# One step later for the scaling of head outputs, and the last output projection as seven products on sums

## The chip, the cores and the metric

The kernel runs on one core of a Trainium2 chip. Its time is the device time of one execution in microseconds (us); before the change the median of three runs is 1851.86 us (1851.43 to 1857.75). The core has a matrix engine (TensorE, PE in the profile), which multiplies a 128x128 tile of weights with up to 512 columns, and three engines for the rest: VectorE (DVE), ScalarE (ACT) and GpSimd (POOL). SyncE (SP) issues every DMA of this kernel, in one order that is fixed when the program is built.

## The reference

A decoder layer on x of 2048 tokens by 1024 channels, all in float32:

```
h        = rms_norm(x, g_pre) * (1 + scale(c)) + shift(c)
pv, pg, hq, hf, hi, hg, mgp, mgh = split(h @ w_in)
branch_a = (pool(pv) @ pool_w * pool_scale * silu(pg)) @ w_pool_o
o        = hgrn2(silu(hq), 1 - f, hi, log f)      # 8 heads of 128, chunks of 64 tokens
branch_b = (rms_norm_per_head(o) * silu(hg)) @ w_hgrn_o
merged   = sigmoid(mgp) * branch_a + sigmoid(mgh) * branch_b
y        = merged @ w_out
x        = x + gate(c) * rms_norm(y, g_post)
```

## The kernel before

The tokens are worked in two passes (p = 0, 1) of 1024, each in two halves (t = 0, 1) of 512 columns, and a half in four tiles (tk) of 128 tokens. A float32 factor is split into a high and a low part that the matrix engine takes at full rate (`split`: ACT casts the high part, DVE subtracts it), and each product is made of three matmuls: high with high, high with low, low with high.

A pass has five stages: the values `hi` for all heads (`v_job`, results in `psV`); eight heads; the projection of branch A (`a_job`, `psA`); the projection and merge of branch B (`b_job`, `psB`, eight jobs j of 128 channels); and the output projection (`y_job`, `psy`). In pass 1 the output projection is four jobs, one for each half of the tokens t and of the output columns nn, and each has 8 blocks k of channels by 4 token tiles by 3 matmuls: 384 matmuls of 512 columns in all.

In a head, three pairs of blocks of `w_in` (tags fq, gp and m) are each made by `quad`: a 2x2 block product over two halves of the channels and two halves of the tokens, in seven products on sums in place of eight. The products leave PSUM in turn; the fourth is copied by ACT (L496, into the bank `pdm`, `pdgp` or `pdfq`), and further matmuls are then added to that bank. Between the products `tick()` moves the two running `hgrn` generators of the head before by one `yield`. Near its end, `hgrn` squares and sums the head output `po` in four tiles of 128 columns (L687, `junk`, sums in `ss`), POOL makes 1/sqrt of `ss` (two small instructions, L390 the second), ACT scales `po` into `on` (L692, four instructions), PE transposes `on` into `pot` three yields later (L698), and DVE and ACT turn it into factors of `b_job`.

Weights come through `take()`, which prepares them LOOK = 4 products ahead. In pass 0 they are loaded, summed and split on DVE and ACT (L172), and the split parts are stored in DRAM scratch (`keep`, L107, from SP). In pass 1 they are loaded back from there (`again`, L194, tag whl, 512 KB in one DMA, one of four buffers). The rows of x for the residual sum are loaded (xr, 256 KB each) in the second quarter of each job with nn = 1.

`y_job` at its end squares each bank on ACT for the row sum (L893, `jy`), multiplies it by the output gate on DVE (L390, `y`), and, when both column halves are there, DVE adds the sums (L902), POOL takes the power (`yss`), and DVE makes y times `yss` plus x (L911). Of the very last token tile ACT and POOL do one of the two halves (L908). The results are stored at once in the last job.

The order on each engine comes from the order in which the code issues its instructions and from a scheduler that places them by the buffers and results they need.

Of the kernel before, what the change touches and what calls it, by code (L numbers as in the profile page):

```python
# [8 lines left out]
F32 = mybir.dt.float32  # L9
# [24 lines left out]
MASK_W = P + 2 * 64 + 5 * NT * 64  # L34
NU = 76
GAP = 5
KINDS = (("m", "gp"), ("gp", "m"))


# [30 lines left out]
def tile_block(ctx: ExitStack, tc: tile.TileContext, x, c, w_ada, b_ada, g_pre, g_post, w_in,  # L70
# [137 lines left out]
    def quad_items(key, oa, ob, keep_it):  # L208
# [37 lines left out]
            return [f0, f1, f2, f3, lambda: one(4, "21"), lambda: one(5, "12"), lambda: one(6, "22")]  # L246
        items.append((7, make))

    early = {}
    pending = []  # L250

# [41 lines left out]


    psa = [ph.tile([P, T], F32, tag=f"ph{i}", name=f"psa{i}") for i in range(2)]
    shv = cst.tile([P, 8], F32, name="shv")
    scv = cst.tile([P, 8], F32, name="scv")

# [90 lines left out]
    def tt(o, a, b, op=MUL, e=None):  # L389
        return (e or V).tensor_tensor(o, a, b, op=op)  # L390
# [131 lines left out]
    def hgrn(p, h, t, cx):  # L522
# [270 lines left out]
        cx["V"][h] = vt  # L793


    def two_out(nm, p, i, t, src, cx, stay):
# [42 lines left out]
    def b_job(p, j, cx):  # L839
        ps = [bank(f"psB{p}_{j}_{t}") for t in range(2)]  # L840
        sm = sig_in(p, j, 1, cx)
        for half in range(2):
            w = take()
            for t in range(2):
                three(ps[t], w, [cx["gG"][4 * half + i, t] for i in range(4)], half == 0, half == 1)
        for t in range(2):
            a, b = cx["a"].pop((j, t)), sm[t]
            tt(b, ps[t], b)
            tt(a, a, b, op=ADD)
            hi, lo = utile(f"mgh{p}_{j}_{t}", F32R), utile(f"mgl{p}_{j}_{t}", F32R)  # L850
            split(a, hi, lo)
            cx["mg"][j, t] = (hi, lo)
# [9 lines left out]
    def y_job(p, t, nn, q, cx):  # L862
# [36 lines left out]
        for tk in range(NT):  # L899
# [5 lines left out]
            for n2 in (0, 1):  # L905
# [9 lines left out]
                else:  # L915
                    outs.append(o)


    cxs = []
    for p in range(NPASS):  # L920
        cx = {k: {} for k in ("sm", "F", "Q", "G", "V", "pw", "Gd", "Pd", "Sd", "gP", "gG", "a", "mg", "x", "xc", "h32",
                              "mv", "y", "yss")}
        cx["Vd"] = dram(f"Vd{p}", [P, 8, D])
        for h in range(NH):
            cx["Gd"][h] = dram(f"Gd{p}_{h}", [P, 2, 2, T])
        for g in range(NG):
            cx["Pd"][g] = dram(f"Pd{p}_{g}", [P, 2, 2, T])
        for j in range(KT):
            for w in range(2):
                cx["Sd"][j, w] = dram(f"Sd{p}_{j}_{w}", [P, 2, T])  # L930
        cxs.append(cx)

    def krow(src, k, o):
        return src[k * P:(k + 1) * P, o:o + T]

    for p in range(NPASS):
        for t in range(2):
            for grp in range(2):
                for k in range(KT):
                    plain_item(("v", grp, k), krow(w_in, k, O_I + grp * T), None, t == 1)  # L940
# [13 lines left out]
        for t in range(2):  # L954
# [50 lines left out]
    for p in range(NPASS):  # L1005
# [3 lines left out]
        if p == 0:  # L1009
# [13 lines left out]
        vj = [(t, grp, q) for t in range(2) for grp in range(2) for q in range(4)]  # L1023
        if p == 0:
            vj = vj[4:]
        for n, (t, grp, q) in enumerate(vj):
# [8 lines left out]
                once(mixes)  # L1035
        while mixes:
            once(mixes)

        v_head(p, 0, cx)
        for h in range(NH):  # L1040
# [17 lines left out]
            steps = []  # L1058

            def tick_in():  # L1060
                tick()
                once(steps)

            quad("fq" + n, cx, fq, tick)
            active.extend(hgrn(p, h, t, cx) for t in range(2))
            tick()
            for i, kind in enumerate(KINDS[h == NH - 1]):
                if kind == "gp":
                    quad("gp" + n, cx, gp, tick)
# [5 lines left out]
                tick()  # L1075
            if p + 1 < NPASS:
                x_stats(8 + h)

        for j in range(KT):
            if j > 0:  # L1080
# [21 lines left out]
        for t in range(2):  # L1102
            for nn in range(2):
                for q in range(4):
                    y_job(p, t, nn, q, cx)
# [29 lines left out]
```

## Time and profile before

| | before |
|---|---|
| median of three runs | 1851.86 us |
| the profiled execution | 1851.48 us |
| its span | 1849.7 us |
| PE busy | 1782.6 us, 96% of the span |
| DVE, ACT, POOL busy | 1089.1, 799.9 and 80.0 us |
| mean DMA rate | 240 GB/s |

The span runs from the first instruction to the last; the execution's own time is 1.8 us more. PE counts as busy while a matmul is under way; matmuls overlap, so a row's mean duration is more than the step from one matmul to the next. The stages of the span: heads of pass 0 lie between 160 and 740 us, most of the heads of pass 1 between 1050 and 1480, the output projection of pass 1 between 1750.46 and 1839.11, and the span ends at 1849.70.

### The profile page before, as it was taken

To read this page: it belongs to the slowest core of one execution; us is meant where nothing else is said; L and a number is where in the kernel's file an instruction comes from. 1 tells how busy PE (TensorE), PEld (TensorE's weight loads), DVE (VectorE), ACT (ScalarE), POOL (GpSimd) and SP (SyncE) were. 2 spreads that over 40 slices of the span, in tenths; PEclk is the share of its full clock that TensorE was granted. 3 is DMA by queue.
4 is the path that set the end of the run, shared out by engine and by line. 5 is a ranking of instruction groups with operands and counts; after the bars stand their busy time and mean duration, and the time that the engine had idled before them with its cause. 6 is when DMAs were issued, how large, how long until landed. Compare 5 with 4: busy or idle time off the path is not lost.

```text
span 1849.7 us, 31713 instructions
## 1 busy us (share of the span) xinstructions
PE 1782.6 (96%) x12053; PEld 1456.7 (79%) x12053; DVE 1089.1 (59%) x2328; ACT 799.9 (43%) x1863; POOL 80.0 (4%) x136
## 2 busy tenths in 40 slices
PE   5999999999999999999999999999999999999997
PEld 4788878878888777787788778878888788788886
DVE  7568877887888884565432255465455456533322
ACT  4746656656556562223322335445344344311111
POOL 1100000000000000000000000000000000000000
PEclk9999999999999999999999999999999999999999
DMA  8697676676767759987887765664764764694476
GB/s 298 233 322 277 221 268 243 231 261 225 266 241 246 247 201 320 361 288 255 295 310 242 246 193 175 224 206 154 234 205 159 231 201 162 233 340 163 141 258 230
DMA packets 236530, 444.19 MB, mean 240 GB/s; under 512 B 18989, under 2 KB 109786, under 8 KB 236378
## 3 DMA queue, kind: packets, MB, share of 16 engines
q1 hardware_dynamic: 236378, 442.17, 69.9%
q8 instruction: 95, 1.56, 0.3%
q14 instruction: 57, 0.47, 0.1%
HBM read 269.61 MB, written 172.49 MB: 239 GB/s over the span
## 4 chain that ended last, share of the span: by engine, by line
PE 79%; ACT 6%; DMA 3%; DVE 3%; POOL 2%; issue 2%; SPq 1%; POOLq 0%; DVEq 0%; ACTq 0%
PE psB L278 9%; PE psV L278 8%; PE psy L278 8%; PE pafq L278 6%; PE pagp L278 6%; PE pam L278 5%; PE pefq L278 5%; PE psA L278 4%; PE pegp L278 4%; PE pem L278 3%; PE psa L278 3%; PE pbfq L278 2%; PE pbm L278 2%; PE pdfq L278 2%; PE pdm L278 2%; PE pbgp L278 2%
## 5 line engine op out<-in xcount | busy, mean ns | idle before, releaser
L172 DVE TENSOR_TENSOR whl<-wr,whl 128x512 fp32r<-128x512 f32 x210 | 143.7, 689 | 83.6 <-ACT whl L172 82.6
L172 ACT CAST whl<-wr 128x512 fp32r<-128x512 f32 x210 | 129.8, 620 | 128.6 <-DMA wr<-in_w_hgrn_o_dram 22.4
L278 PE MATMUL psy<-whl,mgh 128*128 128x512 f32 x512 | 160.1, 393 | 1.4 <-DVE y L390 0.7
L278 PE MATMUL psV<-whl,hB 128*128 128x512 f32 x512 | 161.3, 397 | 0.1
L278 PE MATMUL psB<-Gh,whl 128*128 128x512 f32 x512 | 158.6, 390 | 0.0
L578 DVE COPY_PREDICATED PT<-mask,psa 128x256 f32<-128x256 uint8 x160 | 86.1, 548 | 51.5 <-PE psa L278 51.5
L278 PEld LDWEIGHTS psy<-whl,mgh 128*128 128x128 f32 x512 | 95.0, 188 | 22.5 <-DMA whl<-scr_y 1.7
L278 PEld LDWEIGHTS psB<-Gh,whl 128*128 128x128 f32 x512 | 96.1, 188 | 20.5 <-issue 0.5
L278 PEld LDWEIGHTS psV<-whl,hB 128*128 128x128 f32 x512 | 96.6, 191 | 19.8 <-ACT V L787 0.3
L278 PE MATMUL psV<-whl,lB 128*128 128x512 f32 x256 | 100.8, 395 | 0.0
L278 PE MATMUL psB<-Gl,whl 128*128 128x512 f32 x256 | 100.0, 391 | 0.0
L278 PE MATMUL psy<-whl,mgl 128*128 128x512 f32 x256 | 100.0, 391 | 0.0
L278 PE MATMUL pam<-hT,whl 128*128 128x512 f32 x256 | 87.2, 402 | 0.0
L278 PE MATMUL pagp<-hT,whl 128*128 128x512 f32 x256 | 86.1, 397 | 0.0
L278 PE MATMUL psA<-Ph,whl 128*128 128x512 f32 x256 | 82.6, 397 | 3.4 <-DVE sm L390 1.7
L278 PE MATMUL pafq<-hT,whl 128*128 128x512 f32 x256 | 84.0, 389 | 0.0
L390 DVE TENSOR_TENSOR K<-K,TT 128x256 f32<-128x256 f32 x192 | 81.2, 424 | 1.0 <-PE psa L278 0.9
L278 PEld LDWEIGHTS psa<-X,K 128*32 128x32 f32 x2816 | 50.1, 110 | 29.8 <-issue 21.1
L172 ACT CAST mgh<-sm 128x512 fp32r<-128x512 f32 x32 | 19.7, 620 | 121.3 <-DVE sm L390 121.3
L390 DVE TENSOR_TENSOR y<-psy,gg 128x512 f32<-128x512 f32 x32 | 21.9, 688 | 73.9 <-ACT jy L893 73.7
L278 PE MATMUL psa<-X,K 128*32 128x48 f32 (+2 forms) x2816 | 61.0, 208 | 2.1 <-DVE PT L572 2.1
L572 DVE COPY_PREDICATED PT<-mask,psa 128x256 f32<-128x256 uint8 (+1 forms) x96 | 51.9, 541 | 18.3 <-PE psa L278 18.3
(358 smaller groups left out, 4307.5 us busy)
## 6 DMA issues: line engine op xcount, KB each, us to landing
wr<-in_w_in_dram SPq DMA_DIRECT2D x122, 256.0 KB, 4.4
whl<-scr_y SPq DMA_DIRECT2D x48, 512.0 KB, 4.4
sm<-Sd SPq DMA_DIRECT2D x64, 256.0 KB, 4.3
whl<-scr_v SPq DMA_DIRECT2D x32, 512.0 KB, 3.4
wa<-in_w_ada_dram SPq DMA_DIRECT2D x32, 256.0 KB, 5.4
x<-in_x_dram SPq DMA_DIRECT2D x32, 256.0 KB, 5.5
Vd<-V SPq DMA_DIRECT2D x32, 256.0 KB, 2.4
scr_v<-whl SPq DMA_DIRECT2D x16, 512.0 KB, 2.8
```

The source lines that it names most:

```text
L172: return A.copy(hi, src32), V.tensor_tensor(lo, src32, hi.bitcast(F32), op=SUB)
L278: PE.matmul(o, lhsT=l, rhs=r, start=start, stop=stop, skip_group_check=True)
L390: return (e or V).tensor_tensor(o, a, b, op=op)
L572: V.copy_predicated(dst.rearrange("p (c a) b -> p c a b", c=NT), m.unsqueeze(1).broadcast_to(shp), src.unsqueeze(2).broadcast_to(shp))
L578: V.copy_predicated(dst.rearrange("p (c q) a b -> p c q a b", c=NT), m, src.rearrange("p c (a b) -> p c a b", b=b).unsqueeze(2) .broadcast ...
```

## The change

There are two edits.

In `hgrn` one `yield` is moved from behind the scaling of `po` to a place ahead of it. The transposing into `pot` is issued at the same tick as before; the four scalings are issued one tick later.

The output projection of pass 1 is made as a 2x2 block product too, over the even and the odd 128-row blocks of w_out (2i and 2i+1), the two halves of its columns and the two halves of the tokens. Seven products on sums take the place of eight: B11, B21, T1, T2, T3, B22, T4, each of 4 blocks i by 4 token tiles by 3 matmuls, 336 in all. The sums of the merged branches (T1 to T4) are made in `b_job` of pass 1, on DVE, and split in `step` between the products. The seven sums of w_out are made in `row_factors` during the heads of pass 1: 56 steps, of which `htick` runs one at every second tick; they load w_out (16 DMAs of 256 KB), subtract or add (32 DVE instructions on 128x256), split (56 casts on ACT, 56 subtractions on DVE, 128x256) and store the parts to DRAM scratch (56 stores, from SP). `rows7` loads them back, 28 loads of 512 KB where there were 32, and adds the products on DVE and ACT as their banks become ready. Token half 1 is complete with B22, and half 0 with T4. The flag FAST_V is False, and what it guards is not built.

```
@@ hgrn
         tt(ss, ss, mh[:, 0:NT], op=ALU.pow, e=G)
+        yield
         on = utile("on" + n)
         for cc in range(NT):
             A.activation(on[:, cc * P:(cc + 1) * P], po[:, cc, :], AF.Copy, scale=ss[:, cc:cc + 1])
-        yield
         yield
         yield
@@ new function
+    def row_factors(key, src):
+        steps = []
+        W = T // 2
+        for i in range(4):
+            for c0 in (0, W):
+                r = {}
+                def put(f, nm, i=i, c0=c0, r=r):
...
+                    split(r[nm], hi, lo)
...
+                    store((key, f, i), scr[key, f, i].rearrange("p (z n) -> p z n", z=2)[:, :, c0:c0 + W],
+                          w.bitcast(F32).rearrange("p (z n) -> p z n", z=2))
...
+                steps += [ld, nop, lambda two=two: two((0, "11"), (1, "12")),
+                          lambda two=two, a=sums: two(a, (2, "s1")),
+                          lambda two=two, a=sums2: two(a, (3, "11")),
+                          lambda two=two, a=sums3: two((4, "21"), a),
+                          lambda two=two: two((5, "12"), (6, "22"))]
+        return steps
@@ new function
+    def rows7(name, mv, got, step):
+        acc = [bank(f"ra{name}{tk}") for tk in range(NT)]
+        c, s, u = ([utile(f"r{z}{name}{tk}") for tk in range(NT)] for z in "csu")
+        def done(nm, tk, ps):
+            if nm == "B11":
+                A.copy(c[tk], ps)
+            elif nm == "B21":
+                tt(c[tk], ps, c[tk], op=ADD)
+                got(0, 0, tk, c[tk])
+            elif nm == "T1":
+                A.copy(s[tk], ps)
+            elif nm == "T2":
+                tt(u[tk], ps, s[tk], op=ADD)
+            elif nm == "T3":
+                tt(s[tk], ps, s[tk], op=ADD)
+                got(1, 1, tk, s[tk])
+            elif nm == "B22":
+                tt(u[tk], ps, u[tk], op=ADD)
+                got(0, 1, tk, u[tk])
+            else:
+                got(1, 0, tk, ps)
+        for nm in ("B11", "B21", "T1", "T2", "T3", "B22", "T4"):
+            ps = acc
+            if nm in ("B21", "T1", "B22"):
+                ps = [side(f"rx{name}{nm}{tk}", tk) for tk in range(NT)]
...
@@ b_job, pass 1 (in place of the split)
+                    tt(t1, b12, b11, op=SUB)
+                    tt(b12, b22, b12, op=SUB)
+                    tt(t2, b22, t1, op=SUB)
+                    tt(b21, b21, t2, op=SUB)
@@ new function
+    def y_fast(p, cx):
...
+        def got(n, t, tk, src):
...
+            A.activation(jy, src, AF.Square, scale=1.0 / 32, accum_out=rs[t][tk][:, n:n + 1])
...
+            tt(y, src, cx["gg"][n])
+            ys[t, tk, n] = y
+            if n != 1 - t:
+                return
+            r = rs[t][tk][:, 0:1]
+            V.tensor_scalar(r, r, rs[t][tk][:, 1:2], EPS, op0=ADD, op1=ADD)
+            tt(r, r, mh[:, 0:1], op=ALU.pow, e=G)
...
+                    V.scalar_tensor_tensor(xx, y, r, xx, op0=MUL, op1=ADD)
...
+        def step(nm, i):
...
+            if nm in ("T2", "T3"):
+                t = 1 if nm == "T2" else 0
+                for tk in ((0,), (1,), (2, 3))[i]:
+                    x_in(t, tk)
@@ heads
+        def htick():
+            tick()
+            every[0] += 1
+            if every[0] % 2 == 0:
+                once(behind_heads)
```

The order on ACT in pass 0, while head 2 is being made, from the second half's squares (junk0 to junk3 of `0_1_1`: pass 0, head 1, half 1) to the copy into `pdm`; `on0_1_0` and `on0_1_1` are the scalings of the halves 0 and 1 of head 1. Before:

```order
L687 ACTIVATE junk0_0_1_1_3293,ss0_1_1_3292<-po0_1_1_3282 128x128
L692 ACTIVATE on0_1_0_3277<-po0_1_0_3256,ss0_1_0_3266 128x128 x4
L687 ACTIVATE junk1_0_1_1_3295,ss0_1_1_3292<-po0_1_1_3282 128x128
L608 COPY X8_0_2_0_3518<-sq0_2_0_3105 128x16x16
L687 ACTIVATE junk2_0_1_1_3297,ss0_1_1_3292<-po0_1_1_3282 128x128
L605 COPY X8_0_2_1_3545<-sq0_2_1_3018 128x16x16
L687 ACTIVATE junk3_0_1_1_3299,ss0_1_1_3292<-po0_1_1_3282 128x128
L709 COPY PV0_1_0_3587<-halo_145 128x16
L692 ACTIVATE on0_1_1_3303<-po0_1_1_3282,ss0_1_1_3292 128x128 x4
L496 COPY pdm0_2_3358<-pam0_2_3136 128x512
```

The same place on ACT with the change:

```order
L746 ACTIVATE on0_1_0_3380<-po0_1_0_3258,ss0_1_0_3268 128x128
L740 ACTIVATE junk1_0_1_1_3292,ss0_1_1_3289<-po0_1_1_3279 128x128
L746 ACTIVATE on0_1_0_3380<-po0_1_0_3258,ss0_1_0_3268 128x128
L740 ACTIVATE junk2_0_1_1_3294,ss0_1_1_3289<-po0_1_1_3279 128x128
L746 ACTIVATE on0_1_0_3380<-po0_1_0_3258,ss0_1_0_3268 128x128
L740 ACTIVATE junk3_0_1_1_3296,ss0_1_1_3289<-po0_1_1_3279 128x128
L746 ACTIVATE on0_1_0_3380<-po0_1_0_3258,ss0_1_0_3268 128x128
L661 COPY X8_0_2_0_3520<-sq0_2_0_3107 128x16x16
L746 ACTIVATE on0_1_1_3385<-po0_1_1_3279,ss0_1_1_3289 128x128 x4
L658 COPY X8_0_2_1_3547<-sq0_2_1_3020 128x16x16
L762 COPY PV0_1_0_3589<-halo_145 128x16
L549 COPY pdm0_2_3350<-pam0_2_3138 128x512
```

The scalings of half 0 now alternate with the squares of half 1, both copies into `X8` stand behind the squares, and one of them and the copy into `PV` stand between the second scaling and the copy into `pdm`.

The end of the program on DVE before; the first number in a name `y_1_1_3` is the token half, the second the column half, the third the token tile:

```order
L390 TENSOR_TENSOR y_1_1_2_18070<-psy_1_1_2_17934,gg_1_17488 128x512
L902 TENSOR_SCALAR yss_1_1_17917<-yss_1_1_17917 128x1
L902 TENSOR_SCALAR yss_1_2_17922<-yss_1_2_17922 128x1
L390 TENSOR_TENSOR y_1_1_3_18074<-psy_1_1_3_17935,gg_1_17488 128x512
L911 SCALAR_TENSOR_TENSOR xr_1_1_0_17996<-y_1_0_1_17920,yss_1_1_17917,xr_1_1_0_17996 128x512
L911 SCALAR_TENSOR_TENSOR xr_1_1_1_17997<-y_1_1_1_18066,yss_1_1_17917,xr_1_1_1_17997 128x512
L911 SCALAR_TENSOR_TENSOR xr_1_2_0_18000<-y_1_0_2_17925,yss_1_2_17922,xr_1_2_0_18000 128x512
L911 SCALAR_TENSOR_TENSOR xr_1_2_1_18001<-y_1_1_2_18070,yss_1_2_17922,xr_1_2_1_18001 128x512
L902 TENSOR_SCALAR yss_1_3_17927<-yss_1_3_17927 128x1
L911 SCALAR_TENSOR_TENSOR xr_1_3_1_18005<-y_1_1_3_18074,yss_1_3_17927,xr_1_3_1_18005 128x512
```

And with the change, where `ray` are the banks of T4, `ruy` the sums that B22 completes, and `ys_1_3` the powers of half 1, tile 3:

```order
L443 TENSOR_TENSOR ruy_17833<-ruy_17833,gg_0_17806 128x512
L1054 TENSOR_SCALAR ys_1_3_17817<-ys_1_3_17817 128x1
L443 TENSOR_TENSOR y_0_1_0_18408<-ray_17818,gg_1_17808 128x512
L1063 SCALAR_TENSOR_TENSOR xr_1_3_0_18168<-ruy_17833,ys_1_3_17817,xr_1_3_0_18168 128x512
L1063 SCALAR_TENSOR_TENSOR xr_1_3_1_18170<-rsy_17829,ys_1_3_17817,xr_1_3_1_18170 128x512
L1054 TENSOR_SCALAR ys_0_0_17810<-ys_0_0_17810 128x1
L443 TENSOR_TENSOR y_0_1_1_18428<-ray_17819,gg_1_17808 128x512
L1063 SCALAR_TENSOR_TENSOR xr_0_0_0_18192<-rcy_17822,ys_0_0_17810,xr_0_0_0_18192 128x512
L1063 SCALAR_TENSOR_TENSOR xr_0_0_1_18194<-y_0_1_0_18408,ys_0_0_17810,xr_0_0_1_18194 128x512
L1054 TENSOR_SCALAR ys_0_1_17811<-ys_0_1_17811 128x1
L443 TENSOR_TENSOR y_0_1_2_18444<-ray_17820,gg_1_17808 128x512
L1063 SCALAR_TENSOR_TENSOR xr_0_1_0_18214<-rcy_17823,ys_0_1_17811,xr_0_1_0_18214 128x512
```

The work of half 1 (`xr_1_...`) now stands among the work on T4's first banks, and all four tiles of half 0 are finished behind it.

SP at the start of the heads of pass 1, before and with the change; `scr_` are the scratch tensors, `rfy` the split sums of w_out:

```order
L194 DMA whl_10813<-scr_('m', 0)_0_1474 128x1024
L194 DMA whl_10832<-scr_('m', 0)_1_1498 128x1024
L194 DMA whl_10848<-scr_('m', 0)_2_1519 128x1024
L194 DMA whl_10881<-scr_('m', 0)_3_1555 128x1024
L194 DMA whl_10897<-scr_('m', 0)_4_1575 128x1024
```

```order
L195 DMA whl_10856<-scr_('m', 0)_2_1521 128x1024
L195 DMA whl_10899<-scr_('m', 0)_3_1557 128x1024
L108 DMA scr_y_0_0_10876<-rfy_10873 256x1x256
L108 DMA scr_y_1_0_10881<-rfy_10878 256x1x256
L195 DMA whl_10915<-scr_('m', 0)_4_1577 128x1024
```

The stores of the sums now stand between the loads of the weights, in one queue.

## Rows read from the trace of the kernel before

**Rows 1.** Windows: us, then busy time and instructions by engine, clock, DMA share, GB/s.

```profile
160.00:740.00 580.00, 564.17 (x4554) 460.42 (x4552) 459.27 (x1009) 336.08 (x810) 32.47 (x44) 1.00 0.72 248
1050.00:1480.00 430.00, 423.93 (x3405) 345.81 (x3404) 231.79 (x568) 192.51 (x469) 13.32 (x20) 1.00 0.61 197
1750.46:1839.11 88.65, 88.02 (x385) 71.54 (x383) 18.60 (x33) 10.95 (x31) 2.74 (x5) 1.00 0.74 249
1839.11:1849.70 10.59, 0.00 (x0) 0.00 (x0) 5.58 (x11) 1.41 (x3) 2.88 (x4) 0.70 0.51 198
```

**Rows 2.** Waits of PE, whole span: us in total, times, longest.

```profile
PE pdm L278 <- ACT pdm L496: 14.4, 12, 1.3
...
PE pdgp L278 <- ACT pdgp L496: 3.2, 2, 2.1
PE pot L698 <- ACT on L692: 2.2, 1, 2.2
...
PE pbfq L278 <- DMA whl<-scr_('fq', 0)_3_1388: 1.7, 1, 1.7
```

**Rows 3.** Timeline of ACT in head 2, pass 0: start, us, idle before.

```profile
306.81 1.15 ACT L692 ACTIVATE on<-po,ss 128x128 f32<-128x128 f32 x4 [1.41 <-POOL ss L390]
...
308.08 0.43 ACT L608 COPY X<-sq 128x256 f32<-128x256 f32 x1
...
309.19 0.25 ACT L709 COPY PV<-halo 128x16 f32<-128x16 f32 x1
310.98 1.14 ACT L692 ACTIVATE on<-po,ss 128x128 f32<-128x128 f32 x4 [1.54 <-POOL ss L390]
312.00 0.61 ACT L496 COPY pdm<-pam 128x512 f32<-128x512 f32 x1
```

**Rows 4.** Timeline of PE there.

```profile
312.67 0.50 PE L278 MATMUL pdm<-hT,whl 128*128 128x512 f32 x1 [1.31 <-ACT pdm L496]
```

**Rows 5.** Timeline of DVE at the end.

```profile
1836.06 0.69 DVE L390 TENSOR_TENSOR y<-psy,gg 128x512 f32<-128x512 f32 x1 [18.34 <-ACT jy L893]
...
1837.63 0.75 DVE L911 SCALAR_TENSOR_TENSOR xr<-y,yss,xr 128x512 f32<-128x512 f32 x1 [0.76 <-POOL yss L390]
...
1843.78 0.20 DVE L902 TENSOR_SCALAR yss<-yss 128x1 f32<-128x1 f32 x1
1844.74 0.75 DVE L911 SCALAR_TENSOR_TENSOR xr<-y,yss,xr 128x512 f32<-128x512 f32 x1 [0.76 <-POOL yss L390]
```

**Rows 6.** Costly groups of the page: instructions, busy us, mean ns.

```profile
L172 ACT CAST whl<-wr 128x512 fp32r<-128x512 f32 x210 | 129.8, 620 | 128.6 <-DMA wr<-in_w_hgrn_o_dram 22.4
...
L390 DVE TENSOR_TENSOR K<-K,TT 128x256 f32<-128x256 f32 x192 | 81.2, 424 | 1.0 <-PE psa L278 0.9
...
L390 DVE TENSOR_TENSOR y<-psy,gg 128x512 f32<-128x512 f32 x32 | 21.9, 688 | 73.9 <-ACT jy L893 73.7
```

**Rows 7.** Waits of SP's queue, heads of pass 0 (160 to 700 us).

```profile
SPq L107 <- DVE whl L172: 209.0, 95, 9.1
```

**Rows 8.** Waits of SP's queue, heads of pass 1 (1050 to 1480 us).

```profile
SPq L107 <- ACT c22m L756: 26.4, 6, 4.9
```

**Rows 9.** Tile whl in the output projection: landing of its DMAs.

```profile
DMA to landing us min/median/max: 3.7/4.2/4.5
```

**Rows 10.** Windows of 11 us in the output projection, columns as in rows 1.

```profile
1774.00:1785.00 11.00, 11.00 (x50) 9.09 (x49) 0.00 (x0) 0.00 (x0) 0.00 (x0) 1.00 0.95 325
...
1796.00:1807.00 11.00, 11.00 (x49) 9.02 (x49) 4.29 (x8) 0.00 (x0) 1.04 (x2) 1.00 1.02 339
```

More of the change, by code (lines that the diff above doesn't have):

```diff
@@ L36 @@
 GAP = 5
+FAST_V, FAST_Y = False, True
 KINDS = (("m", "gp"), ("gp", "m"))
@@ L793, in v_head, with mul @@
         cx["V"][h] = vt
+    def rows7(name, mv, got, step):
[23 more added lines that the diff above has]
+                ps = [side(f"rx{name}{nm}{tk}", tk) for tk in range(NT)]
+            def mul(i, w, tk):
+                xh, xl = (z[:, tk * P:(tk + 1) * P] for z in mv[nm, i])
+                mm(ps[tk], xh, w[0], i == 0 and nm in ("B11", "B21", "T1", "B22"), False)
+                mm(ps[tk], xh, w[1], False, False)
+                mm(ps[tk], xl, w[0], False, i == 3)
+            for i in range(2):
+                w = take()
+                for tk in range(NT):
+                    mul(i, w, tk)
+                step(nm, i)
+            ws = [take(), take(LOOK - 1)]
+            for tk in range(NT):
+                for i in (2, 3):
+                    mul(i, ws[i - 2], tk)
+                done(nm, tk, ps[tk])
+            step(nm, 2)
     def two_out(nm, p, i, t, src, cx, stay):
@@ L849, in b_job @@
             tt(a, a, b, op=ADD)
+            if p == NPASS - 1 and FAST_Y:
+                cx["m32"][t, j] = a
+                if t == 0:
+                    part(p, ("B11", "B21")[j % 2] + "m", j // 2, a, cx)
+                elif j % 2 == 1:
+                    b11, b21, b12, b22 = (cx["m32"][z] for z in ((0, j - 1), (0, j), (1, j - 1), (1, j)))
+                    i = j // 2
+                    t1, t2 = utile(f"mt1_{i}"), utile(f"mt2_{i}")
+                    tt(t1, b12, b11, op=SUB)
+                    tt(b12, b22, b12, op=SUB)
+                    tt(t2, b22, t1, op=SUB)
+                    tt(b21, b21, t2, op=SUB)
+                    cx["m32"] = {**cx["m32"], ("T1", i): t1, ("T2", i): t2, ("T3", i): b12, ("B22", i): b22, ("T4", i): b21}
+                    for z in ((0, j - 1), (0, j), (1, j - 1), (1, j)):
+                        del cx["m32"][z]
+                continue
             hi, lo = utile(f"mgh{p}_{j}_{t}", F32R), utile(f"mgl{p}_{j}_{t}", F32R)
@@ L934, in krow, with factor_items @@
         return src[k * P:(k + 1) * P, o:o + T]
+    def factor_items(key):
+        for f in range(7):
+            for i in range(4):
+                items.append((1, lambda f=f, i=i: [again((key, f, i), f"{len(ready)}")]))
     for p in range(NPASS):
-        for t in range(2):
+        if p > 0 and FAST_V:
+            factor_items("v7")
+        for t in range(0 if p > 0 and FAST_V else 2):
             for grp in range(2):
                 for k in range(KT):
-                    plain_item(("v", grp, k), krow(w_in, k, O_I + grp * T), None, t == 1)
+                    plain_item(("v", grp, k), krow(w_in, k, O_I + grp * T), None, t == 1 and not FAST_V)
         for h in range(NH):
@@ L953, in tile_block @@
                            w_hgrn_o[half * T:(half + 1) * T, j * P:(j + 1) * P].rearrange(ko, p=P), P, p == 0)
-        for t in range(2):
+        if p == NPASS - 1 and FAST_Y:
+            factor_items("y7")
+        for t in range(0 if p == NPASS - 1 and FAST_Y else 2):
             for nn in range(2):
@@ L1022, in tile_block, with v_got, v_step @@
             late = [lambda k=k: h_in(0, 1, k, cxs[0]) for k in range(KT)]
-        vj = [(t, grp, q) for t in range(2) for grp in range(2) for q in range(4)]
+        if p > 0 and FAST_V:
+            def v_got(n, t, tk, src):
+                vt = src
+                if (n, t) == (1, 0):
+                    vt = utile(f"V{p}_{t}_{n}_{tk}")
+                    A.copy(vt, src)
+                store("Vd", cx["Vd"][:, t * NT + tk, n * T:(n + 1) * T], vt)
+            def v_step(nm, i):
+                if nm == "B11":
+                    for _ in range(len(late) if i == 2 else 2):
+                        once(late)
+                elif nm == "B21":
+                    for _ in range(2 if i == 2 else 1):
+                        once(mixes)
+            rows7(f"V{p}", cx["mv"], v_got, v_step)
+        vj = [] if p > 0 and FAST_V else [(t, grp, q) for t in range(2) for grp in range(2) for q in range(4)]
         if p == 0:
@@ L1037, in tile_block @@
             once(mixes)
+        psa[:] = [ph.tile([P, T], F32, tag=f"ph{i}", name=f"psa{p}_{i}") for i in range(2)]
+        behind_heads = []
+        if p == 0 and FAST_V:
+            behind_heads += row_factors("v7", w_in[:, O_I:O_I + D])
+        if p == NPASS - 1 and FAST_Y:
+            behind_heads += row_factors("y7", w_out)
+        every = [0]
+        def htick():
[3 more added lines that the diff above has]
+                once(behind_heads)
         v_head(p, 0, cx)
@@ L1074, in tile_block @@
                     quad("m" + n, cx, lambda row, t, u: m_got(p, h, row, t, u, cx), tick_in)
-                tick()
+                htick()
             if p + 1 < NPASS:
                 x_stats(8 + h)
+        while behind_heads:
+            once(behind_heads)
         for j in range(KT):
@@ L1101, in tile_block @@
                         steps.append(lambda p=p, t=t, k=k, nx=nx: h_in(p + 1, t, k, nx))
-        for t in range(2):
+        if p == NPASS - 1 and FAST_Y:
+            y_fast(p, cx)
+        for t in range(0 if p == NPASS - 1 and FAST_Y else 2):
             for nn in range(2):
```

67 lines of the change are left out of this document (62 added, 5 removed).

## The prediction

> **What bounds the kernel now.** I read the windows by stage first, then what the matrix engine waits for, then the timelines at the two places that the diff touches. The windows [rows 1] show a matrix engine that almost never stops: 564.17 of 580 us in the heads of pass 0, 423.93 of 430 in those of pass 1, and 88.02 of 88.65 in the last output projection, at a granted clock of 1.00 in each. So time can come from fewer matmuls, from the few waits that are left, and from the tail, 10.59 us in which PE does nothing at all. DVE, ACT and the DMA queue have room in the projection (18.60, 10.95 us and 0.74 of 88.65). The list of PE's waits [rows 2] names what the first edit can reach: `pdm`, 12 times, 14.4 us; `pdgp`, twice, 3.2; `pot`, once, 2.2. That is 19.8 us, and a wait for a weight load, which the second edit can make worse, stands there once with 1.7.
>
> The profiled execution took 1851.48 us, 0.4 below the median of the runs, 1851.86. The sum is made on 1851.48.
>
> **Fewer matmuls: -11.1.** The stage has 384 matmuls in 88.65 us [rows 1], 0.2309 each, and the change leaves 336. 48 times 0.2309 is 11.1. This needs PE to run through the borders of the products. In each of the seven, the token tiles are finished one after the other over the last half, and three products use other banks than the rest, so that an addition by DVE (0.688 [rows 6]) or a copy by ACT (0.620 for a cast of the same size [rows 6]) has the time of the following tile's six matmuls, 1.4 us, before the bank is wanted. I count no stall. The splits of T1 to T4 and B22 hide under the products: each product is 11.1 us of PE, and ACT and DVE were busy less than a quarter of the stage. If the cover fails once at each of six borders by one DVE instruction, that is 4.1 us.
>
> The Trainium skill (TensorE: Matmul & The Clock Gate, Back-to-back issue gap) gives two spacings for 512 columns, 216 ns for an isolated matmul and 131 ns sustained; as estimates from that page the cut would be 10.4 or 6.3 us. The trace agrees with neither: 0.2309 us is the mean of 384 in this very stage, so the row is used and the page changes no chance.
>
> **The tail: +3.3.** Before, at the end, DVE is free when the last bank is ready (an idle of 18.34 us stands ahead of its first `y` [rows 5]), works through the job, and its last addition of sums starts at 1843.78; POOL's power and the last multiply-add at 1844.74 follow, and the span ends at 1849.70, 5.92 after that addition starts. PE's last matmul ends at 1839.11 [rows 1], so that addition starts 4.67 behind it. Now half 1 is completed by B22, one product before the end, and the order on DVE at the end shows that its 8 multiply-adds, 4 additions of sums and half of the gate products still stand ahead of or among those of T4's banks. Counted from rows: four additions of B22 (0.69), four gate products (0.69), eight multiply-adds (0.75), four small ones (0.20) are 12.3 us, while T4 lasts 11.1 us, and its own tiles add one gate product, one small addition and two multiply-adds each, 2.4 us per tile against the 1.4 in which PE makes a tile. DVE therefore falls behind by about a pair of multiply-adds and a wait for a power (0.76 [rows 5]), and the last addition comes about 3.3 us later behind the last matmul than before. Bounds: 0, if the first three tiles catch up, and +6, if half 1 is still wholly in the way for two tiles more. The value taken is near their middle. The sixteen stores at the end, where there were eight, go out earlier than the last one and are not counted apart.
>
> **The scaling one step later: -5.8.** In the timeline of ACT [rows 3], the second scaling waits 1.54 us for POOL, starts at 310.98, ends about 312.0, and only then comes the copy into `pdm`, 0.61 us; PE waits for that copy 1.31 us, until 312.67 [rows 4]. In the new order the first scaling stands among the squares, without the two copies into X, about 0.84 us (0.43 each [rows 3]). So POOL gets the sums 0.5 to 1.1 us earlier, and so does the second scaling. But the scaling is still ahead of `pdm`, and now one X copy (0.43) and the one of `PV` (0.25) stand between the two, in pass 1 also a cast of the new sums. So the copy into `pdm` comes 0 to 0.9 us earlier; I take 0.3 in each of six places of pass 0 and 0.15 in six of pass 1, 2.7 of the 14.4. `pdgp` is only in the last heads, and there the order has the scalings behind the copy: all 3.2 go, but the transposing for the next `pot` then waits about 0.6 in each of the two, so 2.0. The `pot` wait of 2.2 goes, since the scheduler puts those transposings 28 matmuls later; the first wait of branch A follows closely, and I count half, 1.1. Together 5.8. Bounds: 0, if all of it is given back, a little below by one X copy in each place, and 19.8, if all three waits vanish.
>
> **The sums of w_out in the heads of pass 1: +1.0.** 56 subtractions for splits and 32 sums at 0.424 us for 128x256 [rows 6] are 37.3 us of DVE, and 56 casts at about 0.42 (the nearest row is the DVE one of that size) 23.5 us of ACT. With all of it in the 430 us of the window, DVE goes from 231.79 to 269, 63%. In pass 0, where DVE is at 79% and does the same heads with weight splits besides, PE idles 15.83 of 580 us, 2.7%; in pass 1 6.07 of 430, 1.4% [rows 1]. The upper bound is pass 0's share on 430 us, +5.7; the lower 0. In proportion to the way DVE goes from 54% to 79%, 9 of 25 points, it would be 2.1; I take half of that, since part of pass 0's idle is the `pdm` wait counted above.
>
> **DMA in the last stage: +0.8.** T2 and T3 want 8 loads of x (256 KB) each besides four of weights (512 KB), 4.2 MB in 11.1 us, 378 GB/s. The most that a window of this stage shows is 339 GB/s at a DMA share of 1.02 [rows 10]. At 339 each needs 12.4, 1.3 too long, 2.6 us for both if nothing is ahead; a load lands 4.2 us after its issue [rows 9] and is asked for about three steps (8.3 us) ahead, so most of it is covered: 0.8, between 0 and 2.6.
>
> The Trainium skill (HBM Reference, Specifications (TRN2)) says that a core that streams alone measures about 425 GB/s and one whose neighbour streams too about 358. By estimates from that page T2 and T3 would fit, or be short by 0.6 each, which makes the sum 1838.9 or 1840.1. The trace's own most is 339, nearer the second.
>
> **The sum.** 1851.48 - 11.1 + 3.3 - 5.8 + 1.0 + 0.8 = 1839.7 us, 0.66% below 1851.86. A difference of 0.5%, about what a measurement of this kernel can tell from no change, is 1842.6 or 1861.1.
>
> **The rivals.**
>
> *The heads gain nothing.* If PE still waits for the same copy into `pdm`, since the scaling and now two copies stand ahead of it, and what `pdgp` and `pot` give is paid back by the next wait, the time is 1839.7 + 5.8 = 1845.5, within 0.5%. For it speaks that the new order has the second scaling ahead of `pdm` in every head but the last; against it that POOL gets its sums sooner. 0.20.
>
> *The stores of the sums hold SP's queue, slower.* 56 stores, each waiting for a DVE subtraction, are put between the weight loads of the heads of pass 1 on SP, and SP waits in order. In pass 0 such waits sum to 209.0 us over 95, the longest 9.1 [rows 7]; PE doesn't see them there, since the weights come another way. In pass 1 the longest of the kind is 4.9 [rows 8], and one load was late by 1.7 [rows 2]. A load is asked for three products of 12 matmuls (8.2 us) ahead and lands in about 4.2, so holds beyond 4 us reach PE. If about 40 groups of stores held it on average 0.7 beyond that, the loss is 28 us: 1867.7. It decides for slower from about 0.55 each. Against it: DVE is at 63%, a subtraction follows its cast closely, and the mean hold of pass 0 is 209.0/95 = 2.2, under 4. 0.08.
>
> *All head waits go.* Then 19.8 in place of 5.8: 1825.7. It needs the copy into `pdm` to come over 1.3 us earlier, and the order speaks against it. 0.06.
>
> **Chances and range.** My forecast has 0.66; its own range is 1835 to 1844.5, from the bounds of the tail and the heads, and some 0.88 of it lies below 1842.6. Faster: 0.66 x 0.88 + 0.06 = 0.64. Same: 0.20 + 0.08 = 0.28. Slower: 0.08. The range of 8 in 10 is 1833 to 1848: it leaves out the slower rival, most of the case in which all waits go, and a little of the forecast's and the first rival's ends.
>
> **What would show it.** In the profile after: 336 matmuls in the last projection in about 77.6 us, with no wait of PE on DVE or ACT at the products' borders; between the last matmul and the end of the span 13.9 us; PE's waits for `pdm` about 11.7 in sum, for `pdgp` gone; SP's stores of the sums with holds below 4 us and no new wait of PE for `whl` in the heads of pass 1; in T2 and T3 a DMA share near 1, and a wait or two of PE for the sums' loads under 1 us each. The forecast is wrong if the stage takes over 82 us, if the tail is over 17, or if PE's idle share in 1050 to 1480 is above 2.7%.

## The result and the profile after

The changed kernel takes 1829.36 us (median of 4 runs, 1827.58 to 1831.51) against 1853.35 us before (4 runs). The ratio is 0.9869, 95% interval 0.9851 to 0.9886: 1.3% faster. The forecast was 1839.7 us with a range from 1833 to 1848. The direction was right; the gain is twice the one forecast, and the time lies below the range.

Where it came from is read by stages first. The table goes from the start of the first matmul of a stage to that of the next stage, in the two profiled executions (spans 1849.7 and 1829.7 us); these lie 20.0 us apart, the medians 24.0, so that 4 us of the gain are not in the table.

| stretch | before | after | difference | forecast |
|---|---|---|---|---|
| start to the first `pafq` | 130.9 | 133.4 | +2.5 | 0 |
| heads and branch A, pass 0 | 632.4 | 624.0 | -8.4 | -3.9 |
| branch B, pass 0 | 88.9 | 88.9 | 0 | 0 |
| output projection and values, up to the heads of pass 1 | 185.9 | 186.8 | +0.9 | 0 |
| heads and branch A, pass 1 | 625.3 | 619.8 | -5.5 | -0.9 |
| branch B, pass 1 | 87.0 | 87.0 | 0 | 0 |
| last projection, to its last matmul | 88.65 | 77.42 | -11.2 | -10.3 |
| tail | 10.6 | 12.45 | +1.9 | +3.3 |

The forecast for the heads is split by the waits it spoke of: of the 5.8 the parts of pass 0 are 1.8 for `pdm`, 1.0 for `pdgp`, 1.1 for `pot`; the rest belongs to pass 1, with +1.0 for the sums. The start is not the change's: it lies between 130.7 and 133.4 in all runs below, whatever was edited.

The windows of the changed kernel, which answer to [rows 1] (the first two stages, then the last projection and the tail by its own edges):

```profile
160.00:740.00 580.00, 570.11 (x4580) 465.41 (x4579) 465.29 (x1030) 337.64 (x813) 30.36 (x44) 1.00 0.72 251
1040.00:1470.00 430.00, 425.80 (x3393) 347.10 (x3393) 262.18 (x654) 208.65 (x522) 12.27 (x20) 1.00 0.74 245
1739.83:1817.25 77.42, 76.59 (x337) 62.80 (x335) 41.47 (x70) 25.45 (x58) 2.97 (x4) 1.00 0.71 251
1817.25:1829.70 12.45, 0.00 (x0) 0.00 (x0) 7.23 (x14) 1.41 (x3) 3.45 (x5) 0.61 0.54 211
```

PE idles 9.9 of 580 us where it idled 15.8, and 4.2 of 430 in the heads of pass 1 where it idled 6.1, although DVE there does 30 us more than before. The projection needs 77.42 us; the forecast had 77.6.

PE's waits after, beside [rows 2]:

```profile
PE pdm L325 <- ACT pdm L549: 6.9, 12, 0.9
...
PE psa L325 <- DVE PT L625: 2.7, 3, 1.4
...
PE rxy1B L325 <- ACT hT4m L173: 0.8, 1, 0.8
PE pbfq L325 <- DMA whl<-scr_('fq', 0)_3_1390: 0.7, 1, 0.7
```

The wait for `pdm` has halved, still 12 times; `pdgp` and `pot` are not in the list any more. In the last projection there is one new wait of 0.8 us, at the first matmul of B22, which the view puts down to a cast on ACT. The wait of `psa` for DVE's `PT` (three times, 2.7 us; 2.1 before) comes up again below. The same place on ACT as in [rows 3], head 2 of pass 0:

```profile
308.81 0.37 ACT L746 ACTIVATE on<-po,ss 128x128 f32<-128x128 f32 x1 [1.41 <-POOL ss L443]
...
311.87 1.15 ACT L746 ACTIVATE on<-po,ss 128x128 f32<-128x128 f32 x4 [0.85 <-POOL ss L443]
312.89 0.42 ACT L658 COPY X<-sq 128x256 f32<-128x256 f32 x1
313.19 0.23 ACT L762 COPY PV<-halo 128x16 f32<-128x16 f32 x1
313.30 0.61 ACT L549 COPY pdm<-pam 128x512 f32<-128x512 f32 x1
```

and what PE does with it, as in [rows 4]:

```profile
313.96 0.50 PE L325 MATMUL pdm<-hT,whl 128*128 128x512 f32 x1 [0.60 <-ACT pdm L549]
```

From the first scaling to the second it was 4.17 us (306.81 to 310.98), now 3.06: 1.11 earlier. The two copies that have come between the second scaling and `pdm` start at 312.89 and 313.19, and `pdm` at 313.30: they hold it up by 0.41. So `pdm` comes 0.70 us earlier in this chain, and PE's wait fell by 0.71.

The end on DVE, beside [rows 5]:

```profile
1816.46 0.74 DVE L1063 SCALAR_TENSOR_TENSOR xr<-rsy,ys,xr 128x512 f32<-128x512 f32 x1
1817.12 0.20 DVE L1054 TENSOR_SCALAR ys<-ys 128x1 f32<-128x1 f32 x1
1817.24 0.68 DVE L443 TENSOR_TENSOR y<-ray,gg 128x512 f32<-128x512 f32 x1
...
1823.72 0.21 DVE L1054 TENSOR_SCALAR ys<-ys 128x1 f32<-128x1 f32 x1
1824.59 0.75 DVE L1063 SCALAR_TENSOR_TENSOR xr<-y,ys,xr 128x512 f32<-128x512 f32 x1 [0.66 <-POOL ys L443]
```

PE's last matmul ends at 1817.25. DVE has only just finished half 1 then (the multiply-add of `rsy`) and has begun no more than two tiles of half 0; its last sum of rows starts 6.47 us behind the last matmul, where it was 4.67.

Loads of weights and stores of the sums, heads of pass 1, beside [rows 8] and [rows 9]: first the landing of `whl` between 1040 and 1470 us (shortest, median and longest), then the largest row of holds of SP's queue by stores of the sums (us, times, longest).

```profile
DMA to landing us min/median/max: 3.1/4.2/6.4
```

```profile
SPq L108 <- DVE rfy L173: 37.2, 22, 3.9
```

In the same window before, the landing was 3.2/3.4/3.7. Loads land later, and all rows of such holds come to 54 us, none longer than 3.9, but PE has no new wait for a load there: the one in its list, for `pbfq`, was there before and has shrunk from 1.7 to 0.7.

### The profile page after: what moved, and what is told of

The parts are those of the page before. It is cut to its first block, busy times and chain, and to the rows that moved or that the text cites. A ratio compares the mean times of both kernels' runs of the same rounds, so it can differ in the third digit from the quotient of the medians.

```text
span 1829.7 us, 32049 instructions
## 1 busy us (share of the span) xinstructions
PE 1772.8 (97%) x12005; PEld 1449.7 (79%) x12005; DVE 1148.9 (63%) x2460; ACT 826.9 (45%) x1939; POOL 77.6 (4%) x136
## 4 chain that ended last, share of the span: by engine, by line
PE 79%; ACT 5%; DMA 4%; DVE 4%; POOL 2%; issue 2%; SPq 0%; POOLq 0%; DVEq 0%; ACTq 0%
PE psB L325 9%; PE psV L325 8%; PE pagp L325 7%; PE pafq L325 7%; PE pam L325 5%; PE pefq L325 5%; PE psA L325 4%; PE pegp L325 4%; PE psy L325 3%; PE pem L325 3%; PE psa L325 3%; PE pbfq L325 2%; PE pdfq L325 2%; PE pdm L325 2%; PE pbm L325 2%; PE pbgp L325 2%
## 5 line engine op out<-in xcount | busy, mean ns | idle before, releaser
L325 PE MATMUL psy<-whl,mgh 128*128 128x512 f32 x256 | 80.6, 395 | 0.7 <-DVE y L443 0.7
L443 DVE TENSOR_TENSOR sm<-psB,sm 128x512 f32<-128x512 f32 x32 | 22.0, 688 | 63.8 <-PE psB L325 62.4
L625 DVE COPY_PREDICATED PT<-mask,psa 128x256 f32<-128x256 uint8 (+1 forms) x96 | 52.0, 542 | 12.0 <-PE psa L325 11.9
L325 PEld LDWEIGHTS psA<-Ph,whl 128*128 128x128 f32 x256 | 47.6, 188 | 15.0 <-DMA Ph<-Pd 3.5
L325 PEld LDWEIGHTS psV<-whl,lB 128*128 128x128 f32 x256 | 49.1, 192 | 10.5
L325 PEld LDWEIGHTS pagp<-hT,whl 128*128 128x128 f32 x256 | 48.0, 188 | 10.9 <-issue 0.2
```

Of the source, the lines that this page charges most:

```text
L325: PE.matmul(o, lhsT=l, rhs=r, start=start, stop=stop, skip_group_check=True)
L625: V.copy_predicated(dst.rearrange("p (c a) b -> p c a b", c=NT), m.unsqueeze(1).broadcast_to(shp), src.unsqueeze(2).broadcast_to(shp))
```

## The experiments

Each differs from the kernel named by the edit shown. Times are medians; "before" is the kernel before, run beside it.

**The moved yield alone** (the kernel before, with the first hunk of the change).

> The kernel before with the one moved yield alone (the last projection stays at eight products). Theory A (the scaling that ran ahead of the copies was the whole gain in the heads, and nothing is paid back): PE's waits for the copy into pdm fall from 14.4 to about 7 us, those for pdgp (3.2) and for pot (2.2) go, 13 us in all, so about 1840.4 against a median of 1853.35. Theory B (the scaling gives only the 5.8 us of the forecast, the rest of the gain comes with the seven products, by another order of the heads of pass 1): about 1847.5.

Measured: 1837.90 us against 1853.80, ratio 0.9920 (0.9904 to 0.9937). The heads and branch A take 621.6 us in pass 0 and 621.4 in pass 1, 14.7 less than before together. Its waits:

```profile
PE pdm L278 <- ACT pdm L496: 8.0, 12, 0.9
```

`pdgp` and `pot` are gone from its list. Theory A, and a little more than it said (15.9 by the medians): the yield alone brings most of the whole change, and the forecast's 5.8 is refuted. No wait stands in the list in the place of those that went.

**The seven products alone** (the changed kernel, with the yield back in its old place).

> The changed kernel with the yield put back where it was before (seven products alone). Theory A: only the shorter stage and the longer tail, -11.2 + 1.9, about 1844; PE's waits for pdm 14.4 us as before. Theory B: the rest of the gain is here, about 1835.

Measured: 1847.32 us against 1853.80, ratio 0.9963 (0.9950 to 0.9975), 6.5 us less. The waits in the heads are those of before:

```profile
PE pdm L325 <- ACT pdm L549: 14.5, 12, 1.3
...
PE pdgp L325 <- ACT pdgp L549: 3.5, 2, 2.2
PE pot L751 <- ACT on L745: 2.2, 1, 2.2
```

Its heads take 633.6 and 626.5 us, 1.2 more than before in each pass, also in pass 0, where this kernel does nothing else than the one before; such a difference is scatter. It is also most of what Theory A's 1844 lacks of the 1847.32; the shorter stage (77.57 us) and the longer tail (12.46) are as it said. Theory B falls: what the heads gained doesn't come with the products. The terms for the second edit in the forecast, -11.1 + 3.3 + 1.0 + 0.8, come to -6.0.

**The second scaling behind the copy** (the changed kernel, with an order on ACT that was not there).

```
-        A.copy(d, a)
+        last["pd"] = A.copy(d, a)
...
         for cc in range(NT):
-            A.activation(on[:, cc * P:(cc + 1) * P], po[:, cc, :], AF.Copy, scale=ss[:, cc:cc + 1])
+            with after(last["pd"] if t == 1 else None):
+                A.activation(on[:, cc * P:(cc + 1) * P], po[:, cc, :], AF.Copy, scale=ss[:, cc:cc + 1])
```

> The changed kernel with the second half's scaling ordered behind the copy into pdm (pdgp in the last head) on ACT. Theory A (the copy is late because the scaling and its wait for POOL stand ahead of it): PE's waits for pdm, 6.9 us in the changed kernel, go, and the time falls by about 6.9 to 1822.5. Rival (the next wait takes it: the transposing or the copy's own 0.61 us after pam): pdm falls but the time by less than 2, 1827.5 or more.

Measured: 1818.72 us against 1853.80, ratio 0.9815 (0.9797 to 0.9832), 10.6 less than the changed kernel had. No wait for `pdm` is left; of ACT's in the heads, PE's list holds only 0.2 us for `pmh`, which was there before. The place on ACT, head 2 of pass 0:

```profile
307.99 0.46 ACT L658 COPY X<-sq 128x256 f32<-128x256 f32 x1
308.30 0.25 ACT L763 COPY PV<-halo 128x16 f32<-128x16 f32 x1
308.40 0.63 ACT L549 COPY pdm<-pam 128x512 f32<-128x512 f32 x1
308.99 1.14 ACT L747 ACTIVATE on<-po,ss 128x128 f32<-128x128 f32 x4
```

The copy runs before the scaling, and the scaling no longer shows a wait for POOL, since the copy fills it. So the copy is late because of the order in ACT's queue. But the time fell by more than the 6.9 us of the waits that went, which neither theory had said; the next run shows why.

**The same order with eight products** (the kernel before, with the moved yield and the edit above).

> The kernel before (eight products) with the moved yield and the second half's scaling behind the copies. Theory A (a wait of PE costs more than its row: the matmul behind it starts about 0.3 us later than the row's idle says, since the row counts from the end of the last matmul and the next step is longer too): the waits that go are 19.8 us by their rows, 15 in number, and the time falls by 24 to 27, to about 1827. Theory B (a wait costs its row, the rest of the gain belongs to the seven products): falls by 19.8 or less, 1833.5 or more.

Measured: 1825.05 us against 1853.58, ratio 0.9851 (0.9834 to 0.9868), 28.5 us less by the medians. By stages the heads and branch A take 615.5 and 614.6 us, 27.6 less than before. The rows of the waits that went give 19.8 [rows 2]. Theory B falls; Theory A's 24 to 27 is a little exceeded. Why a wait costs more than its row is seen at one of them, in the kernel before, on PE (the row in question, at 312.67, is in [rows 4]):

```profile
310.96 0.39 PE L278 MATMUL pem<-hB,whl 128*128 128x512 f32 x1
...
313.00 0.40 PE L278 MATMUL pdm<-lT,whl 128*128 128x512 f32 x1
```

Matmuls in a stream start 0.23 us apart. Here the next start comes 1.71 after the last (310.96 to 312.67), and the one after it 0.33 later. That is 1.48 + 0.10 = 1.58 us lost, where the row says 1.31: idle time is counted from the end of a matmul that would have overlapped with the next one. Read from start to start in this way, the 15 waits come to 23.7 us where their rows say 19.8.

Most of the other 3.9 us are in waits that the edit doesn't name. In the kernel before, PE waits for DVE's `PT` three times in pass 0:

```profile
PE psa L278 <- DVE PT L572: 2.1, 3, 1.0
```

This row is gone here, and the wait for `pbfq`'s load, 1.7 before [rows 2], is 0.6. The first goes with the order: it is 1.4 to 3.1 us in the six kernels without it, and at most 0.7 in the five with it. Why DVE comes to `PT` in time there isn't traced. The same two sums answer the question left open above: from the changed kernel to the one with the copy first, the twelve `pdm` waits are worth 10.0 us from start to start, and the wait for `PT` falls from 2.7 to 0.2, against 13.5 us by the stages of the heads and branch A.

**The preparation made twice** (the changed kernel).

```
-            behind_heads += row_factors("y7", w_out)
+            behind_heads += [lambda f=f, g=g: (f(), g()) for f, g in zip(row_factors("y7", w_out), row_factors("z7", w_out))]
```

> The changed kernel with the preparation of the sums of w_out made twice: a second set of the same 56 splits, 32 sums, 16 loads and 56 stores, step by step beside the first, into scratch tensors that nothing reads. Theory A (the preparation is wholly hidden by DVE's and SP's spare time in the heads of pass 1): within 1.5 us of the changed kernel, 1829 to 1831. Theory B (it costs what a loaded DVE costs in pass 0, 1 to 5.7 us per set, made up elsewhere in the changed kernel): 1831 to 1835. Theory C (the stores hold SP's queue near the limit of 4 us, longest hold now 3.9): new waits of PE for weight loads, 1840 or more.

Measured: 1844.99 us against 1853.80, ratio 0.9955 (0.9937 to 0.9972), 15.6 more than the changed kernel by the medians. The heads and branch A of pass 1 take 631.7 us, 11.9 more than in the changed kernel; pass 0 is the same (623.6). New waits of PE there (1031 to 1660 us), and the landing of `whl` between 1040 and 1470:

```profile
PE pbgp L325 <- DMA whl<-scr_('gp', 4)_3_5149: 3.2, 1, 3.2
PE pagp L325 <- ACT c12gp L531: 2.9, 2, 1.5
PE pbgp L325 <- DMA whl<-scr_('gp', 2)_3_3463: 2.6, 1, 2.6
```

```profile
DMA to landing us min/median/max: 3.2/4.7/7.9
```

Theory C by its number and in its kind: weight loads come late. But the longest hold by a store of sums is 4.0 us, hardly more than the 3.9 before, so it is not by longer holds that they come late. The load whose lateness cost 2.6 us was late in being issued, on SP:

```profile
1217.60 0.58 SPq L195 DMA_DIRECT2D whl<-scr_('gp', 2)_2_3417  x1
...
1221.49 1.33 SPq L108 DMA_DIRECT2D scr_y<-rfy  x2
1222.91 1.27 SPq L108 DMA_DIRECT2D scr_z<-rfz  x2
1224.28 0.73 SPq L195 DMA_DIRECT2D whl<-scr_('gp', 2)_3_3463  x1
```

It comes 6.7 us behind the load before it, with nine stores issued between the two, one behind the other and without a pause; in the changed kernel the two loads are issued 1.3 us apart (1214.57 and 1215.86). The price of the first set can't be had from the second, since it isn't linear.

**The second set without its stores** (the kernel above, the second set's 56 stores left out).

```
+                    if key == "z7":
+                        return
                     store((key, f, i), scr[key, f, i].rearrange("p (z n) -> p z n", z=2)[:, :, c0:c0 + W],
```

> The doubled preparation, with the second set's 56 stores left out (its 16 loads, 32 sums and 56 splits stay; nothing reads them). Theory A (the doubled one lost its time to the stores: they hold SP's queue and fill the DMA engines, so weight loads land late): within 3 us of the changed kernel, 1829 to 1832, with no wait of PE for weight loads over 1.5 us. Theory B (DVE and ACT are what the doubling overloads): most of the 15 us stay, 1838 or more.

Measured: 1833.58 us against 1852.33, ratio 0.9900 (0.9885 to 0.9914); heads and branch A of pass 1 622.8 us, 3.0 more than the changed kernel. By the ratios, the 56 stores were worth 0.0055 of about 1853, 10 us, and the 88 DVE instructions, 56 casts and 16 loads 0.0031, 6 us, at the edge of what can be told. Neither theory's number is met (A is missed by 1.6 us, B by 4.4), but A is nearer. Its one load over 1.5 us, 1.7 for `pbfq`, is no witness against it, since the kernel before has the same [rows 2]. Between 1040 and 1470 us, the doubled kernel first, then this one:

```profile
1040.00:1470.00 430.00, 417.95 (x3311) 338.62 (x3312) 290.85 (x740) 221.17 (x572) 13.49 (x20) 1.00 0.84 282
1040.00:1470.00 430.00, 423.93 (x3352) 345.62 (x3352) 290.59 (x741) 223.69 (x577) 12.89 (x20) 1.00 0.77 253
```

DVE is as busy in both, and PE idles 12.1 us in the first and 6.1 in the second. So of the two loads the stores are the dearer. It isn't the waiting of stores in SP's queue that costs: their holds come to 72 us here, the longest 4.2, and to 82 in the doubled kernel, and no load here makes PE wait longer than it did before the change. Whether it is the stores' turns in the queue or the bytes that they move isn't separated: both fell with them.

**Seven products for the values of pass 1 too** (the kernel with the scaling behind the copy, FAST_V set to True).

> The kernel with the scaling behind the copies, and the values of pass 1 as seven products too (the flag FAST_V on): 48 matmuls fewer in the V stage of pass 1, against 56 splits, 32 sums and 56 stores more in the heads of pass 0. Theory A (the preparation hides there too, -11 us): about 1808. Theory B (DVE is at 79% in the heads of pass 0 and SP's stores there already wait for it, so the preparation reaches PE as the doubled one did in pass 1): 1818 or more.

Measured: 1817.45 us against 1852.33, ratio 0.9813 (0.9797 to 0.9828): no difference that can be told from the kernel it was made of (0.9815). Yet theory B isn't right either. The heads and branch A of pass 0, which carry the new preparation, take 616.5 us against 615.2, so it is hidden there. The stretch from the first matmul of the projection of pass 0 to the last of the values shrinks by 5.2 of the expected 11 (838.8 to 1022.0 against 836.6 to 1025.0), with new waits for operands at its start, and the heads and branch A behind it lose 3. The waits that the other kernel has not, or has smaller:

```profile
PE pbfq L325 <- DMA whl<-scr_('fq', 0)_3_1358: 2.6, 1, 2.6
PE raV L325 <- DMA whl<-scr_v: 1.3, 1, 1.3
PE rxV1T L325 <- ACT hT L173: 1.0, 1, 1.0
```

The last two lie in the stretch, 2.3 us of the 5.8 that are missing there. The first lies behind it, at the start of the heads of pass 1, where the other kernel waits 0.5; it is most of the 3 lost there. The rest stays open.

**Work at the end given to ACT and POOL**, in two ways (the kernel with the scaling behind the copy). First five multiply-adds and the sums of rows ahead of the gate products, then two multiply-adds only; the edit shown is the second:

```
-                if n2 == 0 and t == 0 and tk == NT - 1:
+                if (n2 == 0 and t == 0 and tk == NT - 1) or (n2 == 1 and t == 1 and tk >= 2):
```

> The kernel with the scaling behind the copies, and at its end five of the sixteen multiply-adds given from DVE to ACT and POOL (column half 1 of token half 1, and one more tile of half 0), and the sums of rows ahead of the gate products. Theory A (the 1.9 us that the tail grew by are DVE's work on token half 1, left over from B22): the time between the last matmul and the end of the span falls from 12.4 to about 10, the whole to about 1816.5. Rival (the end is set by the stores of the results behind each other): the tail stays at 12 or more.

> The kernel with the scaling behind the copies, and at its end two of the sixteen multiply-adds (column half 1 of token half 1, tiles 2 and 3) given from DVE to ACT and POOL. Theory A (DVE's work left over from B22 sets the end, and in the first attempt POOL's additions only held up its own powers): 1.3 us less on DVE before the last tile, so the time from the last matmul to the end falls from 12.2 to about 11. Theory B (any addition on POOL holds a power that DVE waits for): 12.5 or more. The whole time moves by less than a measurement tells, 1817 to 1820.

Measured: 1818.59 us against 1852.33 (0.9827, 0.9808 to 0.9845) and 1818.81 against 1853.58 (0.9821, 0.9807 to 0.9836), neither told from 0.9815. From the last matmul to the end it is 13.6 us in the first (1803.20 to 1816.8) and 13.5 in the second (1803.10 to 1816.6), 12.5 without the edit (1804.24 to 1816.7). Both theory A's fall: DVE lost more than it was spared. The tail of the first is what its rival said, but the stores of the results were not put to a test. Theory B holds in its number, and in part by its reason: of the two powers below, the second stands behind an addition on POOL, and DVE waits 0.54 for it. In the second, on DVE and then on POOL:

```profile
1800.21 1.27 DVE L443 TENSOR_TENSOR ruy<-ruy,gg 128x512 f32<-128x512 f32 x1 [0.62 <-ACT jy L1048]
1801.40 0.20 DVE L1055 TENSOR_SCALAR ys<-ys 128x1 f32<-128x1 f32 x1
1802.27 0.75 DVE L1064 SCALAR_TENSOR_TENSOR xr<-ruy,ys,xr 128x512 f32<-128x512 f32 x1 [0.66 <-POOL ys L443]
...
1803.65 0.68 DVE L443 TENSOR_TENSOR y<-ray,gg 128x512 f32<-128x512 f32 x1
1804.88 0.75 DVE L1064 SCALAR_TENSOR_TENSOR xr<-rcy,ys,xr 128x512 f32<-128x512 f32 x1 [0.54 <-POOL ys L443]
```

```profile
1799.64 1.29 POOL L443 TENSOR_TENSOR xr<-rsy,xr 128x512 f32<-128x512 f32 x1 [0.84 <-ACT rsy L1061]
1801.68 0.55 POOL L443 TENSOR_TENSOR ys<-ys,mh 128x1 f32<-128x1 f32 x1 [0.75 <-DVE ys L1055]
1803.07 1.27 POOL L443 TENSOR_TENSOR xr<-rsy,xr 128x512 f32<-128x512 f32 x1 [0.84 <-ACT rsy L1061]
1804.29 0.55 POOL L443 TENSOR_TENSOR ys<-ys,mh 128x1 f32<-128x1 f32 x1
```

A gate product that takes 0.68 us elsewhere takes 1.27 where it overlaps with POOL's addition, and a square on ACT now stands behind a scaling, so that DVE waits 0.62 for it and 0.66 for the next power.

## Why the prediction was wrong

**The step that failed** is "The scaling one step later: -5.8". It is worth -14.7 by the stages of the kernel with that edit alone, and -15.9 by its medians; in the changed kernel the heads and branch A take 13.9 less. The mechanism was right: POOL has its sums sooner, and the copy into `pdm` comes sooner by what that gives less what the two copies take. The sizes were off, in two places that matter and one that hardly does:

1. *The gain of each `pdm` copy.* The step had the second scaling 0.5 to 1.1 us earlier, and then set 0.43 + 0.25 against it for the two copies. At the place read it came 1.11 earlier, and the copies cost 0.41: they were priced by the durations of their rows, but ACT's instructions overlap there, and what a following one loses is the distance between starts (0.30 and 0.11). The 0.70 that is left lies inside the step's own 0 to 0.9; the 0.3 and 0.15 that it took came from no row. 0.75 in pass 0 and 0.51 in pass 1 were measured (7.7 to 3.1 us and 6.8 to 3.7 for six waits each). 2.7 should have been 7.5.
2. *What is paid back.* The step gave back 1.2 of `pdgp`'s 3.2 and 1.1 of `pot`'s 2.2. Both waits are gone, and no wait in their place is in the list.
3. *The price of a wait.* The step took the rows at their face. One costs about 0.27 us more, but of the 15 only three have gone in the changed kernel and twelve have become shorter: by rows they fell by 13.0 us, from start to start by 13.6. The full 4 us are won only where all 15 go.

The rival in which all head waits go (1825.7, given 0.06) was nearer to the measured time than the forecast, for the wrong reason: half of the `pdm` wait is still there, and the time came as low as it did partly because the tail, the sums and DMA, which the rival took over from the forecast at +5.1, cost some 3 us less. Its upper bound of 19.8 was no bound either: where the 15 waits did go, they were worth 23.7 from start to start.

**Fewer matmuls: -11.1** is right: 77.42 us for 336, 0.2304 each, -11.2. The step counted no stall at the borders; there is one, of 0.8 us, at the border to B22.

**The tail: +3.3** is right in kind and too large: +1.9. DVE is behind by half 1's last multiply-adds, as the order showed, but its first two gate products of T4 start before the last matmul ends.

**The sums of w_out: +1.0** is 0 within the scatter of a stage. The heads of pass 1 take 1.6 us less in the changed kernel than with the yield alone, and 1.2 more with the products alone than before. The share of DVE's busy time was the wrong measure. With the products alone, DVE works 259.0 us of the window from 1040 to 1470 against 230.3 before, and PE idles 8.2 us against 7.8; with the yield in both kernels, it idles 4.2 with the sums and 4.6 without. The doubled set shows that the room ends soon behind it, and that the stores cost more than DVE's work.

**DMA in the last stage: +0.8** isn't settled. In the windows of T2 and T3, 289 and 317 GB/s were moved and the list of the changed kernel names no wait for a load; the longest landing in the stage is 6.9 us, inside the three steps' 8.3. But one wait stands just behind T3:

```profile
1795.22 0.70 PE L325 MATMUL rxy1B<-whl,hB22m 128*128 128x512 f32 x2 [0.83 <-ACT hT4m L173]
```

The cast of T4's sum that it is put down to is nothing that this matmul reads. All eight kernels with seven products have a wait at this matmul, of 0.4 to 1.5 us, and in five of them it is put down to a load of `whl`. So the forecast's 0.8 may well be this wait, which is inside the 77.42.

**The stores hold SP's queue** (0.08) didn't happen: the longest hold by a store of sums was 3.9 us, just under the 4 that the rival set as its point.

Summed, the terms of the second edit were forecast at -6.0 and measured at -6.5 alone, at -8.5 on top of the yield (1837.90 to 1829.36), and at -6.3 on top of the other order (1825.05 to 1818.72). These differences are between medians taken at different times and good to a few us. By far the larger part of the error, 9 to 10 us, is in the first edit; the tail, the sums and DMA were each set somewhat too high besides.

## What to carry to other kernels

Where an engine waits for an instruction that stands ready behind others in a queue, price what stands ahead of it by the distance between starts and not by durations, and the wait itself from start to start of the engine that waits. Such waits can be worth more than arithmetic: one order in ACT's queue, given by hand, brought 10.6 us on top of the whole change, more than the seven products brought alone (6.5). And work that is hidden once is no evidence that twice as much would be: here the second set cost 15.6 us, and about 10 of them went with its stores, although DVE stayed as busy.

## What the hardware showed beside that

An addition on POOL can slow a product on DVE that runs beside it: a gate product on 128x512 that takes 0.68 us took 1.27 beside an addition of 1.29 us. POOL's addition takes 1.26 with DVE at rest (in the changed kernel at 1825.39), so it lost next to nothing. And it isn't so for every product: the one at 1803.65, whose bank `ray` is in PSUM, took its 0.68 us wholly beside the next addition (1803.07, 1.27 us). This and DVE's three waits are what giving work to POOL and ACT cost in the rows shown.
